# One pool of eight PSUM banks for a whole decoder layer, and a first pair of projections that steps through the contraction in lockstep

## The chip, the core and the metric

The kernel runs on one core of a Trainium2 chip. The metric is the device time of one execution in microseconds (us); lower is better. A core has TensorE (PE, with its weight loads shown apart as PEld), VectorE (DVE), ScalarE (ACT), GpSimd (POOL) and SyncE (SP, which issues most DMAs). Each engine runs its own list of instructions in order, and waits on semaphores for the others. PSUM, where PE writes its results, has eight banks; one bank holds 128 x 512 float32.

## The reference

One layer of a decoder with 512 tokens and 1024 model columns, in float32:

```python
x = x + 0.5 * swiglu(rms_norm(x, ffn1_norm_w), ffn1_w_gate, ffn1_w_up, ffn1_w_down)
h = rms_norm(x, mix_norm_w)
z, xbc, dt_raw, q, k, v = jnp.split(h @ w_in, split_idx, axis=-1)
xbc = jax.nn.silu(causal_dwconv(xbc, conv_w, conv_b))          # 1536 channels, 4 taps
xs, bm, cm = jnp.split(xbc, [1024, 1280], axis=-1)
y_ssd = ssd_chunked(xs, softplus(dt_raw + dt_bias), -exp(a_log), bm, cm, d_skip)
y_ssd = rms_norm(y_ssd * silu(z), ssd_norm_w)                  # per group of 512
q, k = rms_norm(q, q_norm_w), rms_norm(k, k_norm_w)            # 8 heads x 2 x 64
o = rms_norm(diff_attention(q, k, v, lam), attn_subln_w) * 0.8 # softmax(q1 k1) - lam softmax(q2 k2)
x = x + concat([y_ssd, o]) @ w_out
x = x + 0.5 * swiglu(rms_norm(x, ffn2_norm_w), ffn2_w_gate, ffn2_w_up, ffn2_w_down)
```

## The kernel before

Everything is held transposed, 128 channels on the partitions by 512 tokens. Every float32 product is made of three matmuls on operands split in a high and a low part (`mm3`: high x high, high x low, low x high). So a block of 128 weight rows by 512 tokens takes three matmuls, and a channel tile with its eight contraction blocks (k = 0 to 7) takes 24. Weights come in pieces (`piece`), in a fixed list: SP loads a piece into `raw` (three buffers), ACT or POOL makes `whi`, DVE makes `wlo` (four buffers each).

The stages follow each other in the program: feed-forward 1; the projections `xbc` (12 channel tiles, in six pairs, order 8 9, 10 11, 0 1, ... 6 7) with their convolution; the projections z and v mixed with the chunked state-space part (SSD); attention over eight heads mixed with the q and k projections; the output projection `wo`; feed-forward 2. The order on each engine is not that of the program alone: a list scheduler that simulates the engines picks among the instructions whose inputs and buffers are ready in its simulation, the earliest in the program first. So a buffer that is late in the simulation changes the order on the engines.

Steps that matter below:

- End of feed-forward 1. `down` makes the last sums `dn`; for each of eight blocks DVE adds them to x (L362), ACT and DVE make the split operands `xhm` and `xlm` (L236, L237) for the next projections, and POOL adds up squares in `accm` (L247). `finish` then turns `accm` into the norm's factors: PE sums (`psrm`), DVE computes a reciprocal root and a diagonal (L262), PE spreads it (`psbm`), ACT copies it to `rbcm`.
- PSUM. `psum_open` closes the pools in use and opens others on the same banks: eight single banks `P` in the feed-forwards; `A=2, M=2, J=2` in the mixer (an `A` tile is a pair of banks); `J=2, M=4, A=1` in attention.
- `xbc` (L170 to L172 with tile name xbc): the two channel tiles of a pair are written one after the other into one `A` tile. `conv_tile` on DVE (L473 `u`, L480, L482 `a`) empties it, ACT applies SiLU, PE transposes (`xt`, L494), ACT copies the result to `xs` (L496).
- SSD. Per chunk and group `ssd_a` makes the decay matrix `ab` (DMA, eight ReLU L648 and one Exp L649 on ACT, a multiply L653 on DVE), `ssd_o` makes the state's part, and `ssd_d` the diagonal part `pd` (L690), which reads `ab`.
- Attention. Per head `qk_tr` transposes q and k (six tiles qT, khT, klT), `att_s(h, i)` makes the scores `sc` of query block i and their softmax: DVE takes the maximum (L835), ACT exponentiates (L840), POOL and DVE combine the two maps into `pe` (L844, L845). `att_t(h, i)` transposes `pe` on PE (`at`, L853). `att_av` multiplies with v (`o`, 12 matmuls), `att_n` normalizes (`om`). Between these, `fill()` gives PE one part of the q and k projections of later heads (24 matmuls of 256 columns), or of `wo` at the end. In head 6 `y_split` reads the SSD result back and splits it: POOL makes `yh`, DVE makes `yl` (L903).

Of the kernel before, what the change touches and what calls it, by code (L numbers as in the profile page):

```python
# [8 lines left out]
F32 = mybir.dt.float32  # L9
# [29 lines left out]
def hymba_layer(ctx: ExitStack, tc: tile.TileContext, xT, gu1, dn1, wxbc, wdt, wz, wv, wqk,  # L39
                wo, gu2, dn2, cols, rows, out):  # L40
    nc = tc.nc
    V, S, G, PE = nc.vector, nc.scalar, nc.gpsimd, nc.tensor
# [1 line left out]
    const = ctx.enter_context(tc.tile_pool(name="const", bufs=1))  # L44
    wpool = ctx.enter_context(tc.tile_pool(name="wpool", bufs=4))
    dram = ctx.enter_context(tc.tile_pool(name="dram", bufs=1, space=DRAM))
    psum = {}

    def psum_open(**bufs):

        for cm, _ in reversed(list(psum.values())):
            cm.__exit__(None, None, None)
        psum.clear()
        for tag, n in bufs.items():
            cm = tc.tile_pool(name=f"ps{tag}", bufs=n, space=PSUM)
            psum[tag] = (cm, cm.__enter__())

    def pA(name):
        return psum["A"][1].tile([P, 2, T], F32, tag="A", name=name)

    def pM(name, dt=F32):
        return psum["M"][1].tile([P, T], dt, tag="M", name=name)

    def pJ(name):
        return psum["J"][1].tile([P, T], F32, tag="J", name=name)

    ctx.callback(psum_open)
    psum_open(P=8)
# [90 lines left out]
    def piece(ahead=2):  # L159
        i = taken[0]  # L160
        taken[0] += 1
        prep(i + 1 + ahead)
        return ready[i]

    def blk(w, k, width=P):
        return w[:, k * width:(k + 1) * width]

    def mm3(ps, w, k, xh, xl, start, stop):
        hi, lo = blk(w[0], k), blk(w[1], k)
        PE.matmul(ps, lhsT=hi, rhs=xh, start=start, stop=False)  # L170
        PE.matmul(ps, lhsT=hi, rhs=xl, start=False, stop=False)  # L171
        PE.matmul(ps, lhsT=lo, rhs=xh, start=False, stop=stop)  # L172
# [15 lines left out]
    identb = const.tile([P, P], BF16, name="identb")  # L188
# [30 lines left out]
    class Normed:  # L219
# [27 lines left out]
                (V if first else G).tensor_add(self.acc, sq, self.acc)  # L247

        def finish(self):
            pt = pP if "P" in psum else pM  # L250
            ps = pt(f"psr{self.name}")
            for j in range(NB):
                PE.matmul(ps[:, j:j + 1], lhsT=blk(self.acc, j), rhs=ones[:, 0:1], start=True, stop=True)
            self.v = tiny.tile([P, NB], F32, tag="nv", name=f"v{self.name}")
            V.tensor_scalar(self.v, ps[:, :NB], 1.0 / 1024, EPS, op0=ALU.mult, op1=ALU.add)
            self.r = tiny.tile([P, NB], F32, tag="nr", name=f"r{self.name}")
            rsqrt(self.r, self.v, [P, NB], "n")
            dg = self.acc.rearrange("p (a b) -> p a b", a=NB)
            pb = pt(f"psb{self.name}")
            sh = [P, NB, P]  # L260
            yield
            V.tensor_tensor(dg, ident.unsqueeze(1).to_broadcast(sh), self.r.unsqueeze(2).to_broadcast(sh),  # L262
                            op=ALU.mult)
            PE.matmul(pb, lhsT=ones, rhs=self.acc, start=True, stop=True)
            S.copy(self.rbc, pb)
            yield
# [146 lines left out]
    nm = [None]  # L413
# [7 lines left out]
    ffn(n1, x1, done1, "1", PARTS1, EARLY1)  # L421
    nm = nm[0]
    xpool_cm.__exit__(None, None, None)
    psum_open(A=2, M=2, J=2)


    mix_cm = tc.tile_pool(name="mix", bufs=1)
# [136 lines left out]
    for n, pair in enumerate(order):  # L564
        if n == 2:
            pt_dt = dt_proj()
            small_consts()
        ps = pA(f"xbc{n}")
        for i in range(2):
            w = piece()  # L570
            for k in range(KD):
                mm3(ps[:, i, :], w, k, nm.xh[:, k, :], nm.xl[:, k, :], k == 0, k == KD - 1)
            if n == 0 and i == 0:
                fin = nm.finish()
                next(fin)
            elif n == 0:
                next(fin)
        if n == 3:
            dt_finish(pt_dt)
        for t, dst in pend:  # L580
            conv_tr(t, dst)
        pend = [(t, conv_tile(t, ps[:, i, :])) for i, t in enumerate(pair)]
    last_conv = pend

    hr = const.tile([P, NB], F32, name="hr")
# [79 lines left out]
    def ssd_o(c, g, m, xdt, xdd, y):  # L665

        hs = slice(g * 8, g * 8 + 8)
        sh = [P, 8, 64]
        cs = slice(c * P, (c + 1) * P)
        pd = pds[c, g] = pA(f"pd{c}{g}")  # L670
        if c > 0:
            PE.matmul(pd[:, 1, :], lhsT=cT[:, g, cs], rhs=state[:, g, :], start=True, stop=True)
            yo = sb.tile(sh, F32, tag="yo", name="yo", bufs=1)
            V.tensor_tensor(yo, sview(pd[:, 1, :]), ea[:, c, hs].unsqueeze(2).to_broadcast(sh), op=ALU.mult)
            V.tensor_add(y, y, yo)
        if c < NB - 1:
            pst = pM(f"st{c}{g}")
            PE.matmul(pst, lhsT=btok[:, c, g, :], rhs=xdd.rearrange("p a b -> p (a b)"), start=True, stop=True)
            st = sview(state[:, g, :])
            if c == 0:  # L680
                S.copy(st, sview(pst))
            else:
                V.tensor_tensor(st, st, cdec[:, c, hs].unsqueeze(2).to_broadcast(sh), op=ALU.mult)
                V.tensor_add(st, sview(pst), st)

    def ssd_d(c, g, m, xdt, xdd, y):

        pd = pds.pop((c, g))
        for h in range(8):
            PE.matmul(pd[:, 0, h * 64:(h + 1) * 64], lhsT=m[:, h, :], rhs=xdt[:, h, :], start=True, stop=True)  # L690
        V.tensor_tensor(y, sview(pd[:, 0, :]), y, op=ALU.add)
        zt = sview(sz[:, c, g * 512:(g + 1) * 512])
        V.tensor_mul(zt, zt, y)
        S.activation(y, zt, AF.Square, accum_out=ssq[g][:, c:c + 1])
# [411 lines left out]
```

## Time and profile before

| | us |
|---|---|
| median of 3 runs (lowest, highest) | 1196.5 (1195.9, 1197.11) |
| the profiled execution | 1194.4 |
| its span, first to last instruction | 1192.3 |
| outside the span | 2.1 |
| PE busy | 1160.0 |
| DVE busy | 895.1 |
| ACT busy | 569.6 |

The profile shows one execution, 2.1 us below the median of the runs. Matmuls are pipelined: the duration of one overlaps the next, so a stretch of back-to-back matmuls is counted in matmuls per us, not in durations. Every row names the engine, the line of the kernel, the operation, what it writes and reads, and in brackets how long the engine was idle before it and what ended that.

### The profile page before, as it was taken

What the parts mean: (1) busy time and instruction counts of PE and PEld (TensorE: products, weight loads), DVE (VectorE), ACT (ScalarE), POOL (GpSimd) and SP (SyncE); (2) the same over time, 40 slices, a digit from 0 to 9 for tenths busy, and PEclk for the clock granted to TensorE, in tenths of its full rate; (3) what the DMA queues carried; (4) which work ended last, traced back from release to release, by engine and by line L of the source; (5) the groups of instructions that cost most, each with busy time, mean ns of one, the idle gap of its engine ahead of it and who ended that gap; (6) DMA issues with size and microseconds to landing.
All of it is one profiled execution on the core that took longest, in us unless ns stands there. A gap on an engine that the chain in (4) does not pass through costs nothing.

```text
span 1192.3 us, 18991 instructions
## 1 busy us (share of the span) xinstructions
PE 1160.0 (97%) x7483; PEld 1033.1 (87%) x7483; DVE 895.1 (75%) x1485; ACT 569.6 (48%) x991; POOL 155.2 (13%) x178
## 2 busy tenths in 40 slices
PE   8999999999998999999999998899999999999998
PEld 6889999999986788999988896688789999999997
DVE  6988787887675875976588988636599888787863
ACT  5433443343353448973366766735244444343331
POOL 1000000000022000000346656423000000000000
PEclk9999999999998999999999999999999999999999
DMA  6223333233253223423221103025213333333232
GB/s 231 89 76 98 100 108 99 92 111 106 89 186 127 77 90 107 142 89 110 88 70 48 60 19 124 27 63 211 80 62 105 108 111 98 110 107 102 96 108 84
DMA packets 42393, 119.56 MB, mean 100 GB/s; under 512 B 4608, under 2 KB 9920, under 8 KB 42304
## 3 DMA queue, kind: packets, MB, share of 16 engines
q1 hardware_dynamic: 41024, 114.15, 29.8%
q0 software_dynamic: 1280, 4.20, 1.0%
q8 instruction: 59, 0.97, 0.3%
q14 instruction: 30, 0.25, 0.1%
HBM read 112.00 MB, written 6.32 MB: 99 GB/s over the span
## 4 chain that ended last, share of the span: by engine, by line
PE 83%; DVE 8%; ACT 4%; issue 2%; POOL 1%; DMA 1%; SPq 0%; ACTq 0%; POOLq 0%; DVEq 0%
PE s L327 9%; PE s L326 9%; PE s L328 9%; PE dn L170 6%; PE dn L172 6%; PE dn L171 6%; PE gu L170 3%; PE gu L172 3%; PE gu L171 3%; PE wo L172 2%; PE wo L170 2%; PE wo L171 2%; PE xbc L170 2%; PE xbc L171 2%; PE xbc L172 2%
## 5 line engine op out<-in xcount | busy, mean ns | idle before, releaser
L128 ACT CAST whi<-raw 128x1024 fp32r<-128x1024 f32 (+2 forms) x204 | 176.6, 868 | 309.5 <-PE s L327 121.7
L129 DVE TENSOR_TENSOR wlo<-raw,whi 128x1024 fp32r<-128x1024 f32 (+3 forms) x225 | 226.5, 1010 | 113.4 <-ACT whi L128 102.0
L327 PE MATMUL s<-al,whi 128*128 128x256 f32 x952 | 265.0, 279 | 0.0
L326 PE MATMUL s<-ah,whi 128*128 128x256 f32 x952 | 263.4, 279 | 0.0
L328 PE MATMUL s<-ah,wlo 128*128 128x256 f32 x952 | 262.4, 279 | 0.0
L327 PEld LDWEIGHTS s<-al,whi 128*128 128x128 f32 x952 | 178.7, 188 | 2.1
L326 PEld LDWEIGHTS s<-ah,whi 128*128 128x128 f32 x952 | 178.3, 188 | 2.0
L328 PEld LDWEIGHTS s<-ah,wlo 128*128 128x128 f32 x952 | 177.1, 187 | 0.1
L128 ACT CAST whi<-tw 128x1024 fp32r<-128x1024 f32 x68 | 70.4, 1051 | 141.0 <-PE s L327 65.6
L170 PE MATMUL dn<-h,whi 128*128 128x512 f32 x352 | 137.5, 394 | 0.0
L172 PE MATMUL dn<-h,wlo 128*128 128x512 f32 x352 | 137.5, 392 | 0.0
L171 PE MATMUL dn<-h,whi 128*128 128x512 f32 x352 | 136.8, 389 | 0.0
L129 DVE TENSOR_TENSOR wlo<-tw,whi 128x1024 fp32r<-128x1024 f32 x68 | 82.0, 1220 | 2.9 <-ACT whi L128 2.8
L172 PEld LDWEIGHTS dn<-h,wlo 128*128 128x128 f32 x352 | 66.1, 188 | 14.6
L171 PEld LDWEIGHTS dn<-h,whi 128*128 128x128 f32 x352 | 66.1, 188 | 12.7
L170 PEld LDWEIGHTS dn<-h,whi 128*128 128x128 f32 x352 | 66.1, 188 | 12.2
L603 PE MATMUL qk<-whi,xhm 128*128 128x256 f32 x256 | 74.1, 289 | 0.3 <-DVE kf L781 0.3
L605 PE MATMUL qk<-whi,xlm 128*128 128x256 f32 x256 | 73.4, 287 | 0.0
L604 PE MATMUL qk<-wlo,xhm 128*128 128x256 f32 x256 | 73.1, 286 | 0.0
L362 DVE SCALAR_TENSOR_TENSOR x<-dn,x 128x512 f32<-128x512 f32 x64 | 44.1, 688 | 35.3 <-PE dn L172 34.8
L170 PE MATMUL gu<-xh,whi 128*128 128x512 f32 x160 | 65.0, 406 | 3.4 <-POOL whi L126 2.3
L172 PE MATMUL gu<-xh,wlo 128*128 128x512 f32 x160 | 63.7, 398 | 0.0
(293 smaller groups left out, 2529.1 us busy)
## 6 DMA issues: line engine op xcount, KB each, us to landing
raw<-in_gu SPq DMA_DIRECT2D x86, 512.0 KB, 3.5
raw<-in_dn SPq DMA_DIRECT2D x48, 384.0 KB, 3.1
raw<-in_wqk SPq DMA_DIRECT2D x16, 512.0 KB, 3.7
raw<-in_wxbc SPq DMA_DIRECT2D x12, 512.0 KB, 3.6
raw<-in_wo SPq DMA_DIRECT2D x10, 512.0 KB, 4.4
raw<-in_dn SPq DMA_DIRECT2D x16, 256.0 KB, 2.6
raw<-in_wz SPq DMA_DIRECT2D x8, 512.0 KB, 3.5
raw<-in_wv SPq DMA_DIRECT2D x8, 512.0 KB, 3.6
```

The lines of the kernel that those rows point to most:

```text
L128: S.copy(hi[:, a:b], raw[:, a:b])
L129: V.tensor_sub(lo[:, a:b], raw[:, a:b], hi[:, a:b].bitcast(F32))
L170: PE.matmul(ps, lhsT=hi, rhs=xh, start=start, stop=False)
L171: PE.matmul(ps, lhsT=hi, rhs=xl, start=False, stop=False)
L172: PE.matmul(ps, lhsT=lo, rhs=xh, start=False, stop=stop)
L326: PE.matmul(ps, lhsT=hi, rhs=ah[:, i, a], start=i == 0, stop=False)
L327: PE.matmul(ps, lhsT=hi, rhs=al[:, i, a], start=False, stop=False)
L328: PE.matmul(ps, lhsT=lo, rhs=ah[:, i, a], start=False, stop=i == 3)
L362: V.scalar_tensor_tensor(x[d], ps, 0.5, x[d], op0=ALU.mult, op1=ALU.add)
L603: PE.matmul(o, lhsT=xh, rhs=hi, start=k == 0, stop=False)
L604: PE.matmul(o, lhsT=xh, rhs=lo, start=False, stop=False)
L605: PE.matmul(o, lhsT=xl, rhs=hi, start=False, stop=k == KD - 1)
```

## The change

The pools `P`, `A`, `M`, `J` and their closing and opening are gone. One pool of eight single banks serves the whole program; `pM`, `pJ` and `pP` are now one function, and each pair of banks becomes two tiles. Three places follow from it: the scores of query blocks 2 and 3 are two tiles, so their maximum is taken by two reductions in place of one (16 more DVE instructions in all); the SSD tile `pd` becomes two tiles; `wo4` and `wo5` are two tiles. Apart from that, the first pair of `xbc` tiles steps through k in lockstep: for each k three matmuls of the one tile and three of the other. `finish` is split otherwise: `psrm` after the first pair, `psbm` after the first tile of the second pair, and the first pair's convolution comes after that.

```diff
-    psum = {}
-
-    def psum_open(**bufs):
...
-    def pA(name):
-        return psum["A"][1].tile([P, 2, T], F32, tag="A", name=name)
+    pspool = ctx.enter_context(tc.tile_pool(name="psum", bufs=8, space=PSUM))
 
     def pM(name, dt=F32):
-        return psum["M"][1].tile([P, T], dt, tag="M", name=name)
...
+        return pspool.tile([P, T], dt, tag="P", name=name)
+
+    pJ = pP = pM
...
-    psum_open(A=2, M=2, J=2)
...
-        ps = pA(f"xbc{n}")
+        ps = [pP(f"xbc{n}{i}") for i in range(2)]
+        if n == 0:
+            ws = [piece(), piece()]
+            for k in range(KD):
+                for p_, w in zip(ps, ws):
+                    mm3(p_, w, k, nm.xh[:, k, :], nm.xl[:, k, :], k == 0, k == KD - 1)
+            fin = nm.finish()
+            next(fin)
+            first_ps = ps
+            continue
         for i in range(2):
             w = piece()
             for k in range(KD):
-                mm3(ps[:, i, :], w, k, nm.xh[:, k, :], nm.xl[:, k, :], k == 0, k == KD - 1)
-            if n == 0 and i == 0:
-                fin = nm.finish()
+                mm3(ps[i], w, k, nm.xh[:, k, :], nm.xl[:, k, :], k == 0, k == KD - 1)
+            if n == 1 and i == 0:
                 next(fin)
-            elif n == 0:
-                next(fin)
+                pend0 = [(t, conv_tile(t, p_)) for t, p_ in zip(order[0], first_ps)]
...
-        pend = [(t, conv_tile(t, ps[:, i, :])) for i, t in enumerate(pair)]
+        pend = [(t, conv_tile(t, ps[i])) for i, t in enumerate(pair)]
+        if n == 1:
+            pend = pend0 + pend
...
-        pd = pds[c, g] = pA(f"pd{c}{g}")
+        pd = pds[c, g] = [pP(f"pd{c}{g}{i}") for i in range(2)[:2 if c else 1]]
...
         if i < 2:
-            ps = pM(f"sc{h}{i}").rearrange("p (a b) -> p a b", a=2)
+            ps2 = pM(f"sc{h}{i}").rearrange("p (a b) -> p a b", a=2)
+            ps = [ps2[:, t] for t in range(2)]
         else:
-            ps = pA(f"sc{h}{i}")
+            ps = [pM(f"sc{h}{i}{t}") for t in range(2)]
...
-        V.tensor_reduce(nmx, ps[:, :, :K], axis=AX, op=ALU.max, negate=True)
+        if i < 2:
+            V.tensor_reduce(nmx, ps2[:, :, :K], axis=AX, op=ALU.max, negate=True)
+        else:
+            for t in range(2):
+                V.tensor_reduce(nmx[:, t:t + 1], ps[t][:, :K], axis=AX, op=ALU.max, negate=True)
...
-    psum_open(J=2, M=4, A=1)
...
-    pa = pA("wo4")
-    wo_ps[4], wo_ps[5] = pa[:, 0, :], pa[:, 1, :]
+    wo_ps[4], wo_ps[5] = pJ("wo4"), pJ("wo5")
...
-    psum_open(P=8)
```

The scheduler, given other buffers, puts the mixer's instructions in another order on every engine. PE has the same matmuls in both. In its new order nearly every part stands as the program has it, where before parts were slipped between each other. Three places follow.

PE, start of the SSD part, from the last transpose of the convolution (`xt7`) to the first diagonal part (`pd00`, now `pd000`); z0_1 and z1_0 are halves of the projections z, `cb` and `st` small products of the SSD part. Before:

```order
L494 MATMUL xt7_4206<-ident_92,xst_4154 128x128 x4
L604 MATMUL z0_1_4277<-wlo_4067,xhm_3280 128x256
...
L644 MATMUL cb00_4250<-cT_3505,bT_3504 128x128
L678 MATMUL st00_4335<-xdd_4266,btok_3506 128x512
...
L644 MATMUL cb10_4377<-cT_3505,bT_3504 128x128
...
L678 MATMUL st10_4477<-xdd_4393,btok_3506 128x512
L603 MATMUL z1_1_4447<-whi_4165,xhm_3280 128x256
...
L644 MATMUL cb20_4515<-cT_3505,bT_3504 128x128
L690 MATMUL pd00_4334<-xdt_4263,ab_4248 128x64 x8
```

Now:

```order
L473 MATMUL xt7_4202<-ident_92,xst_4150 128x128 x4
L632 MATMUL cb00_4246<-cT_3495,bT_3494 128x128
L591 MATMUL z0_1_4273<-whi_4062,xhm_3280 128x256
...
L666 MATMUL st00_4331<-xdd_4262,btok_3496 128x512
...
L632 MATMUL cb10_4373<-cT_3495,bT_3494 128x128
L591 MATMUL z1_0_4346<-whi_4161,xhm_3280 128x256
...
L678 MATMUL pd000_4330<-xdt_4259,ab_4244 128x64 x8
L591 MATMUL z1_1_4443<-whi_4161,xhm_3280 128x256
```

Between `xt7` and the first `pd` stood 110 matmuls of z (14, 24, 24 and 48), two `st` and three `cb`; now 96 (48, 24 and 24), one `st` and two `cb`.

PE, first head, from its scores of query blocks 0 and 1 (sc00, sc01) to the transpose of its first softmax (`at00`); qk2_0 is a half of the projections of head 2. Before:

```order
L832 MATMUL sc01_5970<-cmask_106,identb_99 128x128
L830 MATMUL sc02_6046<-khT_5897,qT_5890 128x384
...
L832 MATMUL sc02_6046<-cmask_106,identb_99 128x128
...
L603 MATMUL qk2_0_6070<-whi_6066,xhm_3280 128x256
L604 MATMUL qk2_0_6070<-wlo_6067,xhm_3280 128x256
L605 MATMUL qk2_0_6070<-whi_6066,xlm_3281 128x256
L853 MATMUL at00_6042<-ident_92,pe_5962 128x128
```

Now:

```order
L821 MATMUL sc00_5942<-cmask_106,identb_99 128x128
L820 MATMUL sc01_5960<-klT_5915,qT_5901 128x256
L821 LDWEIGHTS identb_99
L821 MATMUL sc01_5960<-cmask_106,identb_99 128x128
L846 MATMUL at00_6032<-ident_92,pe_5952 128x128
L819 MATMUL sc020_6036<-khT_5887,qT_5880 128x384
```

The six matmuls of sc02 and 48 of qk2_0 that stood between the scores of block 0 and `at00` are now behind `at00`. In heads 1 to 5 the same stretch held 36, 43, 40, 36 and 47 matmuls of 256 columns, most of them of q and k projections, and the 12 of `o`; now 16, 9, 24, 11 and 24, and the 12.

DVE, head 6, from the maximum of its scores of block 0 (`nmx<-sc60`) to its first `pe`. Before:

```order
L835 TENSOR_REDUCE nmx_7870<-sc60_7863 128x2
L857 TENSOR_TENSOR atL_5676<-at53_7856,atH_5675 128x4x128
L836 TENSOR_TENSOR nmx_7870<-nmx_7870,qrs_7443 128x2
...
L842 RECIPROCAL l_7892<-l_7892 128x2
L836 TENSOR_TENSOR nmx_8004<-nmx_8004,qrs_7629 128x2
L845 SCALAR_TENSOR_TENSOR pe_7873<-pe_7873,l_7874 128x128
```

Now:

```order
L825 TENSOR_REDUCE nmx_7884<-sc60_7877 128x2
L850 TENSOR_TENSOR atL_5678<-at53_7870,atH_5677 128x4x128
...
L896 TENSOR_TENSOR yl_7988<-yt_7989,yh_7987 128x1024
...
L896 TENSOR_TENSOR yl_7988<-yt_7993,yh_7987 128x1024
L835 RECIPROCAL l_7906<-l_7906 128x2
L909 TENSOR_TENSOR ol2_7930<-oT_5676,oh2_7929 128x512
...
L896 TENSOR_TENSOR yl_7988<-yt_7997,yh_7987 128x1024
L838 SCALAR_TENSOR_TENSOR pe_7887<-pe_7887,l_7888 128x128
```

Three of the four `yl` now stand between the maximum and `pe`; before, all stood ahead of the maximum. On PE, 8 matmuls of 256 columns and the 12 of `o` stand between the scores of block 1 of head 6 and `at60`; before, 21 of `wo` (512 columns) and the 12. In head 7 PE now has 19 matmuls of `wo` and the 12 of `o` in this place, where before it had the 12 alone.

## Rows read from the trace of the kernel before

**Rows 1.** The page: busy time of each engine, share of the span, instructions.

```profile
PE 1160.0 (97%) x7483; PEld 1033.1 (87%) x7483; DVE 895.1 (75%) x1485; ACT 569.6 (48%) x991; POOL 155.2 (13%) x178
```

**Rows 2.** The waits of PE: who waited for whom, us in total, times, longest.

```profile
PE xbc L170 <- DVE x L362: 5.6, 1, 5.6
PE at L853 <- DVE pe L845: 3.5, 5, 1.1
PE wo L171 <- DVE yl L903: 2.7, 3, 1.4
PE at L853 <- DVE l L843: 2.6, 1, 2.6
...
PE qT L810 <- POOL qs L789: 2.2, 1, 2.2
PE sc L830 <- ACT pe L840: 1.5, 1, 1.5
...
PE at L853 <- ACT atH L856: 1.2, 1, 1.2
...
PE at L853 <- DVE klT L813: 0.8, 1, 0.8
PE pd L690 <- DVE ab L653: 0.8, 1, 0.8
```

**Rows 3.** The timeline from feed-forward 1 to xbc: start, us, instruction.

```profile
363.11 0.76 PE L170 MATMUL xbc<-xhm,whi 128*128 128x512 f32 x1 [5.57 <-DVE x L362]
364.02 1.76 DVE L237 SCALAR_TENSOR_TENSOR xlm<-x,col,xhm 128x512 fp32r<-128x512 f32 x1
374.40 0.95 PE L253 MATMUL psrm<-ones,accm 128*128 128x1 f32 x8
377.90 0.69 DVE L262 TENSOR_TENSOR accm<-ident,rm 128x512 f32<-128x512 f32 x1
```

**Rows 4.** Stretches: length, busy PE, PEld, DVE, ACT, POOL; clock; DMA, GB/s.

```profile
363.00:368.00 5.00, 4.89 (x12) 3.86 (x13) 2.78 (x2) 1.36 (x2) 3.71 (x6) 0.50 0.58 197
563.00:573.00 10.00, 10.00 (x88) 10.00 (x87) 2.15 (x4) 4.27 (x7) 0.00 (x0) 1.00 0.70 210
583.00:588.00 5.00, 4.95 (x32) 4.95 (x33) 2.38 (x9) 3.32 (x10) 1.93 (x2) 0.66 0.32 111
650.00:700.00 50.00, 47.28 (x370) 42.02 (x369) 45.71 (x95) 36.01 (x93) 32.33 (x31) 1.00 0.14 43
765.00:770.00 5.00, 5.00 (x18) 3.93 (x17) 1.99 (x5) 3.08 (x6) 2.28 (x3) 0.72 0.02 3
```

**Rows 5.** The timeline of PE from the last xt to the first pd.

```profile
452.02 0.60 PE L494 MATMUL xt<-ident,xst 128*128 128x128 f32 x4
470.05 2.00 PE L690 MATMUL pd<-xdt,ab 128*128 128x64 f32 x16 [0.77 <-DVE ab L653]
```

**Rows 6.** The timeline of DVE: block 0's maximum and pe, heads 0, 6, 7.

```profile
595.38 0.41 DVE L835 TENSOR_REDUCE nmx<-sc 128x2 f32<-128x256 f32 x1
...
600.90 0.35 DVE L845 SCALAR_TENSOR_TENSOR pe<-pe,l 128x128 f32<-128x128 f32 x1
...
741.40 0.42 DVE L835 TENSOR_REDUCE nmx<-sc 128x2 f32<-128x256 f32 x1
...
744.84 0.34 DVE L845 SCALAR_TENSOR_TENSOR pe<-pe,l 128x128 f32<-128x128 f32 x1
...
757.79 0.42 DVE L835 TENSOR_REDUCE nmx<-sc 128x2 f32<-128x256 f32 x1 [0.40 <-PE sc L832]
...
762.95 0.35 DVE L845 SCALAR_TENSOR_TENSOR pe<-pe,l 128x128 f32<-128x128 f32 x1
```

**Rows 7.** DVE's groups by shape: busy us, mean ns, idle before.

```profile
L129 DVE TENSOR_TENSOR wlo<-raw,whi 128x1024 fp32r<-128x1024 f32 x106 | 132.4, 1250 | 32.2 <-ACT whi L128 22.4 <-PE psb L264 4.8 <-POOL whi L126 3.3
...
L903 DVE TENSOR_TENSOR yl<-yt,yh 128x1024 fp32r<-128x1024 f32 x4 | 6.3, 1582 | 0.0
...
L835 DVE TENSOR_REDUCE nmx<-sc 128x2 f32<-128x512 f32 x8 | 5.4, 677 | 0.0
```

More of the change, by code (lines that the diff above doesn't have):

```diff
@@ L46, in hymba_layer @@
     dram = ctx.enter_context(tc.tile_pool(name="dram", bufs=1, space=DRAM))
-    psum = {}
-    def psum_open(**bufs):
[L51 to L56, printed above, removed]
-    def pA(name):
-        return psum["A"][1].tile([P, 2, T], F32, tag="A", name=name)
-    def pM(name, dt=F32):
-        return psum["M"][1].tile([P, T], dt, tag="M", name=name)
-    def pJ(name):
-        return psum["J"][1].tile([P, T], F32, tag="J", name=name)
-    ctx.callback(psum_open)
-    psum_open(P=8)
-    def pP(name):
-        return psum["P"][1].tile([P, T], F32, tag="P", name=name)
+    pspool = ctx.enter_context(tc.tile_pool(name="psum", bufs=8, space=PSUM))
+    def pM(name, dt=F32):
+        return pspool.tile([P, T], dt, tag="P", name=name)
+    pJ = pP = pM
     def ffn_plan(parts, early):
@@ L249, in finish @@
         def finish(self):
-            pt = pP if "P" in psum else pM
-            ps = pt(f"psr{self.name}")
+            ps = pP(f"psr{self.name}")
             for j in range(NB):
@@ L258, in finish @@
             dg = self.acc.rearrange("p (a b) -> p a b", a=NB)
-            pb = pt(f"psb{self.name}")
+            pb = pP(f"psb{self.name}")
             sh = [P, NB, P]
@@ L669, in ssd_o @@
         cs = slice(c * P, (c + 1) * P)
-        pd = pds[c, g] = pA(f"pd{c}{g}")
+        pd = pds[c, g] = [pP(f"pd{c}{g}{i}") for i in range(2)[:2 if c else 1]]
         if c > 0:
-            PE.matmul(pd[:, 1, :], lhsT=cT[:, g, cs], rhs=state[:, g, :], start=True, stop=True)
+            PE.matmul(pd[1], lhsT=cT[:, g, cs], rhs=state[:, g, :], start=True, stop=True)
             yo = sb.tile(sh, F32, tag="yo", name="yo", bufs=1)
-            V.tensor_tensor(yo, sview(pd[:, 1, :]), ea[:, c, hs].unsqueeze(2).to_broadcast(sh), op=ALU.mult)
+            V.tensor_tensor(yo, sview(pd[1]), ea[:, c, hs].unsqueeze(2).to_broadcast(sh), op=ALU.mult)
             V.tensor_add(y, y, yo)
@@ L689, in ssd_d @@
         for h in range(8):
-            PE.matmul(pd[:, 0, h * 64:(h + 1) * 64], lhsT=m[:, h, :], rhs=xdt[:, h, :], start=True, stop=True)
-        V.tensor_tensor(y, sview(pd[:, 0, :]), y, op=ALU.add)
+            PE.matmul(pd[0][:, h * 64:(h + 1) * 64], lhsT=m[:, h, :], rhs=xdt[:, h, :], start=True, stop=True)
+        V.tensor_tensor(y, sview(pd[0]), y, op=ALU.add)
         zt = sview(sz[:, c, g * 512:(g + 1) * 512])
@@ L824, in att_s @@
         if i < 2:
-            ps = pM(f"sc{h}{i}").rearrange("p (a b) -> p a b", a=2)
+            ps2 = pM(f"sc{h}{i}").rearrange("p (a b) -> p a b", a=2)
+            ps = [ps2[:, t] for t in range(2)]
         else:
-            ps = pA(f"sc{h}{i}")
+            ps = [pM(f"sc{h}{i}{t}") for t in range(2)]
         for t in range(2):
             qT, khT, klT = qkT[h][3 * t:3 * t + 3]
-            PE.matmul(ps[:, t, :kc], lhsT=blk(qT, i), rhs=khT[:, :kc], start=True, stop=False)
-            PE.matmul(ps[:, t, :kc], lhsT=blk(qT, i), rhs=klT[:, :kc], start=False, stop=False)
-            PE.matmul(ps[:, t, i * P:K], lhsT=identb, rhs=cmask, start=False, stop=True)
+            PE.matmul(ps[t][:, :kc], lhsT=blk(qT, i), rhs=khT[:, :kc], start=True, stop=False)
+            PE.matmul(ps[t][:, :kc], lhsT=blk(qT, i), rhs=klT[:, :kc], start=False, stop=False)
+            PE.matmul(ps[t][:, i * P:K], lhsT=identb, rhs=cmask, start=False, stop=True)
         rs = qk[h][i // 2][0][:, i % 2, :]
         nmx = tiny.tile([P, 2], F32, tag="nmx", name="nmx")
-        V.tensor_reduce(nmx, ps[:, :, :K], axis=AX, op=ALU.max, negate=True)
+        if i < 2:
[3 more added lines that the diff above has]
+                V.tensor_reduce(nmx[:, t:t + 1], ps[t][:, :K], axis=AX, op=ALU.max, negate=True)
         V.tensor_mul(nmx, nmx, rs[:, 0:2])
@@ L839, in att_s @@
         for t in range(2):
-            S.activation(pe[:, t, :K], ps[:, t, :K], AF.Exp, bias=nmx[:, t:t + 1], scale=rs[:, t:t + 1],
+            S.activation(pe[:, t, :K], ps[t][:, :K], AF.Exp, bias=nmx[:, t:t + 1], scale=rs[:, t:t + 1],
                          accum_out=l[:, t:t + 1])
@@ L1037, in hymba_layer @@
     xn_cm.__exit__(None, None, None)
-    psum_open(P=8)
     def done2(d):
```

## The prediction

> **What bounds the kernel now.** The page comes first: PE is busy for 1160.0 us of a span of 1192.3 [rows 1], DVE for 895.1. The matmuls are the same before and after, so the time can only change by three things: how long PE waits, at which clock it works, and whether another engine becomes the bound. The waits of PE come second [rows 2]. One stands out: 5.6 us of the first `xbc` matmul for DVE's last addition `x` (L362). The others that the change touches lie in attention (`at`, `sc`, `wo`) or at the seams ahead of it (`z`, `pd`, `qT`), each between 0.7 and 3.5 us. The stretches come third [rows 4]. In the 5 us from 363 the granted clock was 0.50, right behind the 5.57 us of idle PE; it was 0.66 behind the 2.20 us before `qT` and 0.72 behind the 2.60 us in the last head. So each long wait is paid twice: 5.0 x 0.50 = 2.5 us, 5.0 x 0.34 = 1.7 us and 5.0 x 0.28 = 1.4 us come on top. I price the clock behind a new long wait at 1.5 us, from the two shorter ones, with 0 and 2.5 as bounds. From 650 to 700, in the middle of attention, DVE is busy for 45.71 of 50 us: there it hardly has room.
>
> **The boundary: a gain of 8.1 us.** The first `xbc` tile is a pair of banks in a new pool, and gets them only when the last user of the old pool is done, DVE's `x` of block 7. Its operands for k = 0 were there long before. In one pool of single banks the two first tiles take the banks of the earliest `dn` sums, so PE goes on at 363.11 - 5.57 = 357.54 [rows 3]. There the lockstep matters: k = 7 is needed only after 42 matmuls of 512 columns. A matmul of 256 columns goes by in 10 / 88 = 0.114 us [rows 4], one of 512 in twice that, so k = 7 is reached at 357.54 + 42 x 0.228 = 367.1. Its `xlm` is ready at 364.02 + 1.76 = 365.8 [rows 3]. Nothing is left to wait for: -5.6 for the wait and -2.5 for the clock. If the clock fell all the same, the gain would be 5.6, which is the lower bound.
>
> **The norm's factors: a loss of 1.6 us.** From `psrm` to the end of DVE's diagonal there pass 377.90 + 0.69 - 374.40 = 4.2 us [rows 3]; in the new order of DVE two `wlo` of 128 x 1024 are slipped into that chain, 1.25 us each [rows 7]. PE has 24 matmuls of 512 columns in this time, 5.5 us; 4.2 + 2 x 1.25 - 5.5 gives +1.2, bounds 0 (the `wlo` find room in the chain's own pauses) and 2.6 (with the clock). The product of the time steps now stands directly behind its own result's copy on ACT; PE's waits for an operand made just before are 0.8 at `pd` and `klT` [rows 2], bounds 0 and 0.8, taken as +0.4.
>
> **The SSD's start: a loss of 4.4 us.** From the end of the last `xt` to the first `pd` there are 470.05 - 452.62 = 17.4 us [rows 5]. This is a chain through ACT and DVE (the decay matrix, its table and exponential, then `ab`), which the change leaves as it is. PE filled it with z, and waited 0.8 us at its end [rows 2]. Now 14 matmuls of z, one `st` and one `cb` fewer stand there: 14 x 0.114 = 1.6 us, and for the two others, by the 16 float32 matmuls of 64 columns that took 2.00 us [rows 5], 512 columns at 1.0 and 128 at 0.25. PE so waits 2.9 us more, 3.7 in all at `pd`, which is longer than the waits of 2.2 and 2.6 behind which the clock fell: +2.9 + 1.5 = +4.4. Bounds: 1.6 (only z counts, no clock) and 5.4 (2.9 + 2.5).
>
> **The first head: a loss of 5.0 us.** Block 0's softmax takes 600.90 + 0.35 - 595.38 = 5.9 us from its maximum to the end of `pe` [rows 6]. Before, 48 matmuls of projections and a third block's scores covered most of that, and PE waited 1.8 us (two of the five waits of `at` for `pe`, [rows 2]). Now `at00` stands directly behind `sc01`, whose six matmuls cover some 0.6 us. A wait of 5.9 - 0.6 = 5.3, less 1.8, with a clock of 1.5: +5.0. Bounds: 1.4 (the shortest chain of the eight heads, 3.8 us [rows 6], and no clock) and 6.0.
>
> **Heads 1 to 5: a loss of 0.6 us.** In head 7 before, the 12 matmuls of `o` alone stood in this place; its chain took 762.95 + 0.35 - 757.79 = 5.5 us [rows 6] and PE waited 2.6 [rows 2], so `o` and what goes with it cover 2.9. With 16, 9, 24, 11 and 24 more at 0.114 the covers are now 4.7, 3.9, 5.6, 4.2 and 5.6 us. The mean chain of the eight heads is 4.9; I take 5.2, between that and head 7's. Waits of 0.5, 1.3, 0, 1.0 and 0 give 2.8 against 1.0 before (3.5 less 1.8 in head 0 and 0.7 in head 6, [rows 2]). I count the 1.2 us for `atH` as absorbed, since PE now stands still a little earlier and the late engines catch up: +1.8 - 1.2 = +0.6. Bounds: -2.2 (no such wait left) and +1.8.
>
> **Head 6: a loss of 2.4 us.** Three `yl` of 1.58 us [rows 7] now stand on DVE between the maximum and `pe`: a chain of 4.9 + 4.7 = 9.6 against a cover of 2.9 + 8 x 0.114 = 3.8, a wait of 5.8 and a clock of 1.5. The waits that it replaces are 2.7 for `yl`, 1.5 for `pe` at `sc` [rows 2] and 0.7 for `pe` at `at`: 7.3 - 4.9 = +2.4. Bounds: -0.2 (a chain of 3.8, as this head had [rows 6], and no clock) and +3.4.
>
> **The tail: a gain of 4.8 us.** In head 7 the 19 matmuls of `wo` now lie between scores and transposes: 19 x 0.228 = 4.3 and 2.9 cover 7.2 us against a chain of 5.5. The 2.6 and 0.8 us [rows 2] and the clock's 1.4 [rows 4] go.
>
> **Taken as nothing.** The 16 split maxima: one of 512 takes 0.68 [rows 7], two of 256 take 0.41 to 0.42 each [rows 6], so a split costs 0.15 and all of them 2.3 us of DVE, hidden behind PE as long as PE waits for block 0 and not for blocks 2 and 3; on the path it would be +2.3. The Trainium skill (Perfetto Trace Analysis, Optimizing Scalar/DVE Operations) has some 125 ns of overhead for a DVE instruction on PSUM and advises larger operations where the engine is saturated: by an estimate from it 16 x 0.125 = 2.0 us, a loss if DVE is the bound. `qT` keeps its 2.2 us, bounds -2.2 and +1.7. Feed-forward 2 and the projections v and q, k run as before.
>
> **The sum.** -8.1 + 1.2 + 0.4 + 4.4 + 5.0 + 0.6 + 2.4 - 4.8 = +1.1. The profiled execution took 1194.4 us, so 1195.5; the median of the runs shown, 1196.5, lies 2.1 above that execution. The forecast is 1197.6 us: what is gained at the seams is given back where the transposes now stand close behind the softmax.
>
> **The rivals.** *B, faster: the chains get shorter.* With eight banks free in any stage, scores and projections need not wait for a pair or for a pool, DVE and ACT get their input sooner, and the softmax takes its shortest time of 3.8 us in every head. No new wait then lasts long enough for the clock. The terms become -8.1, 0, +0.4, +2.9, +1.4 (head 0), -2.2 (heads 1 to 5), -0.2 and -4.8: -10.6, or 1185.9 us. For it: one head of the eight did have 3.8 [rows 6], and the largest wait of all was one for banks. Against it: the other waits of [rows 2] are all for an operand that DVE, ACT or POOL makes, not for a bank. The Trainium skill (Perfetto Trace Analysis, Optimization Strategy) says that a repeated gap on the engine that should be busy "can mean there isn't enough SBUF/PSUM for the next tile to be allocated"; by that rule B would be the case. The trace agrees at one place, the 5.57 us of the boundary, which do not repeat.
>
> *C, slower: DVE becomes the bound in attention.* It is busy for 91% of the time from 650 to 700 [rows 4], and in the new order each chain starts closer to the work it must share DVE with. With chains 1.5 us longer than taken the waits of heads 1 to 5 are 2.0, 2.8, 1.1, 2.5 and 1.1, or 6.7 more; heads 0 and 6 get 1.5 each, and two of the waits reach the clock, 3.0. That is +12.7 on the forecast, 1210.3 us. It decides from a chain of some 5.5 us on, where 0.3 us in each of seven heads already makes the kernel slower by 0.2%. Against it: while PE waits, DVE works off what is late.
>
> *D, no change at the boundary.* If another operand of the first pair is late (DVE is working without a pause there), the 8.1 us stay: 1205.7 us. Against it: the weights' `wlo` are made two pieces ahead.
>
> **How the numbers follow.** A measurement of this kernel can tell about 0.2%, 2.4 us, from no change. The forecast has a chance of 0.52, B 0.27, C 0.13, D 0.08. The forecast's own range is 1192 to 1203, from its bounds at half their width; about 0.11 of its 0.52 lie below 1194.1, 0.25 within 2.4 us of 1196.5, and 0.16 above 1198.9. B is faster, C and D are slower: 0.38 faster, 0.25 the same, 0.37 slower. The range reaches from B's time to two thirds of the way to C's, 1185 to 1206; it leaves out C's upper half, a part of D and what lies below B, together some 2 in 10.
>
> **What would show it.** The wait of `xbc` for `x` is gone from the list of PE's waits, and the clock at 358 to 368 is 1.0 (otherwise D). New waits stand at `psbm` (about 1.2 us), `pd` (3.7), the first `at` (5.3) and the `at` of head 6 (5.8), the latter three with a clock of 0.5 to 0.7 behind them. The last head shows no wait over 1 us. If the waits of `at` sum to under 7 us and no clock falls in attention, B holds; if heads 1 to 5 wait over 6 us, C. The prediction is wrong above all if PE waits for a bank at a place that the order does not show, since tiles now come free in one ring, or if the chain ahead of `pd` follows PE instead of ACT.

## The result, and the profile after

The changed kernel takes 1209.7 us (median of 4 runs, 1209.4 to 1210.8) against 1196.2 us before in the same rounds: a ratio of 1.012, 95% interval 1.0107 to 1.0132. The forecast was 1197.6, the range ended at 1206. The span grew from 1192.3 to 1207.7 us.

The page of the changed kernel, busy times:

```profile
PE 1165.2 (96%) x7483; PEld 1040.2 (86%) x7483; DVE 890.7 (74%) x1501; ACT 571.8 (47%) x993; POOL 155.0 (13%) x178
```

Against [rows 1] DVE is busy for 4 us less although it has 16 instructions more. PE has as many matmuls as before. So the loss is in waits and in the clock. PE's waits after (who waited for whom, us in total, times, longest):

```profile
PE at L846 <- DVE pe L838: 17.9, 6, 5.5
PE at L846 <- DVE l L836: 6.2, 1, 6.2
PE pd L678 <- DVE ab L641: 4.7, 1, 4.7
...
PE o L861 <- DVE atL L850: 1.9, 2, 0.9
PE qT L798 <- POOL qs L777: 1.4, 1, 1.4
...
PE klT L798 <- POOL kl L780: 0.9, 1, 0.9
PE klT L798 <- ACT pe L833: 0.7, 1, 0.7
PE psdtT L494 <- ACT dtr L491: 0.7, 1, 0.7
PE khT L798 <- ACT kh L779: 0.6, 1, 0.6
PE qk L591 <- ACT pe L833: 0.2, 1, 0.2
```

The reader sees three things beside [rows 2]. The wait of `xbc` for `x` is gone, and so are the 2.6 us of the last head and the 2.7 us of `wo` for `yl`. The wait at `pd` is 4.7 us where it was 0.8. And the transposes `at` wait 24.1 us for the softmax, in seven of eight heads, where these waits summed to 6.1.

The stretch behind the boundary, where the wait is gone, and those behind the new waits (length, busy PE, PEld, DVE, ACT, POOL, then the granted clock, DMA share, GB/s):

```profile
363.00:368.00 5.00, 5.00 (x26) 4.13 (x25) 2.45 (x3) 1.69 (x5) 3.37 (x6) 1.00 0.53 165
...
455.00:460.00 5.00, 2.40 (x11) 2.40 (x12) 1.65 (x2) 4.99 (x15) 0.00 (x0) 0.61 0.34 105
460.00:465.00 5.00, 5.00 (x24) 5.00 (x25) 3.45 (x5) 2.78 (x6) 0.00 (x0) 0.50 0.29 105
465.00:470.00 5.00, 5.00 (x30) 4.04 (x29) 2.61 (x5) 4.93 (x16) 0.00 (x0) 0.87 0.02 5
...
583.00:588.00 5.00, 4.17 (x23) 4.18 (x24) 3.39 (x8) 2.25 (x6) 2.74 (x3) 0.50 0.12 48
...
598.00:603.00 5.00, 2.53 (x10) 1.92 (x11) 3.48 (x17) 3.20 (x12) 0.85 (x2) 0.65 0.36 105
603.00:608.00 5.00, 5.00 (x29) 4.73 (x29) 2.41 (x6) 1.79 (x5) 1.86 (x2) 0.67 0.01 3
650.00:655.00 5.00, 4.19 (x15) 2.77 (x16) 3.80 (x12) 1.89 (x6) 0.62 (x2) 0.66 0.28 104
675.00:680.00 5.00, 2.79 (x10) 1.61 (x10) 4.83 (x15) 1.62 (x6) 2.31 (x2) 0.80 0.63 210
680.00:685.00 5.00, 5.00 (x34) 4.14 (x33) 1.59 (x6) 3.65 (x10) 3.36 (x3) 0.86 0.01 3
700.00:705.00 5.00, 2.33 (x16) 1.77 (x15) 4.40 (x13) 4.16 (x15) 2.09 (x3) 1.00 0.53 171
750.00:755.00 5.00, 1.97 (x8) 1.38 (x8) 3.97 (x9) 0.52 (x3) 4.24 (x4) 0.50 0.77 226
755.00:760.00 5.00, 5.00 (x19) 3.49 (x18) 4.92 (x12) 3.54 (x7) 0.00 (x0) 0.85 0.48 133
```

At the boundary the clock is 1.00, where it was 0.50. Elsewhere busy PE times what the clock lacks of 1 is, as an estimate, what the clock took. Behind `pd` that is 2.40 x 0.39 + 5.00 x 0.50 + 5.00 x 0.13 = 4.1 us, in head 0 it is 2.5, in heads 2 and 3 it is 1.4 and 1.3, and in head 6 it is 1.7. Head 4's wait of 2.67 us is not followed by a lower clock (1.00 from 700).

### The profile page after: what moved, and what is told of

Its sections match the earlier page's. It is cut to its first block, busy times and chain, and to the rows that moved or that the text cites. A ratio compares the mean times of both kernels' runs of the same rounds, so it can differ in the third digit from the quotient of the medians.

```text
span 1207.7 us, 18994 instructions
## 1 busy us (share of the span) xinstructions
PE 1165.2 (96%) x7483; PEld 1040.2 (86%) x7483; DVE 890.7 (74%) x1501; ACT 571.8 (47%) x993; POOL 155.0 (13%) x178
## 4 chain that ended last, share of the span: by engine, by line
PE 87%; DVE 6%; ACT 3%; issue 2%; POOL 1%; DMA 1%; SPq 0%; ACTq 0%; POOLq 0%; DVEq 0%
PE s L307 9%; PE s L306 9%; PE s L308 9%; PE dn L151 7%; PE dn L153 7%; PE dn L152 7%; PE gu L151 3%; PE gu L153 3%; PE gu L152 3%; PE wo L151 2%; PE wo L153 2%; PE wo L152 2%; PE xbc L151 2%; PE xbc L153 2%; PE xbc L152 2%
## 5 line engine op out<-in xcount | busy, mean ns | idle before, releaser
L153 PEld LDWEIGHTS dn<-h,wlo 128*128 128x128 f32 x352 | 66.1, 188 | 14.6
L591 PE MATMUL qk<-whi,xhm 128*128 128x256 f32 x256 | 77.9, 304 | 0.2 <-ACT pe L833 0.2
```

What stands on the lines that cost most here:

```text
L591: PE.matmul(o, lhsT=xh, rhs=hi, start=k == 0, stop=False)
```

## The experiments

**Which stage.** Two theories stood at the start. The order theory: PE's `at` and `pd` now stand too close behind the chains that feed them, so the loss is in the SSD part and in attention. The ring theory: a pool of single banks itself costs. In the first run the boundary and the `xbc` stage are the changed ones, and the SSD part and attention have the pools and maxima of before.

```diff
     last_conv = pend
+    psum_open(A=2, M=2, J=2)
...
+    psum_open(J=2, M=4, A=1)
     fillers += [qk_proj(h) for h in range(1, 8)]
```

> The changed boundary and xbc stage alone; the SSD part and attention run with the pools of before, and their maxima are not split. Order theory (the loss of the changed kernel is that PE's transposes and diagonal products now stand too close behind their softmax and decay chains, in the SSD part and in attention): PE's order in attention is that of before, so only the gain at the boundary is left, about 7.8 us, and some 2 to 4 us of waits at pd, for more z stands ahead of it: 1185 to 1190 us. Ring theory (a pool of single banks is itself what costs, by waits for banks or by the clock): the xbc stage has such a pool too, so the gain at the boundary is given back within the stage, 1194 to 1198 us.

Measured: 1187.9 us, ratio to before 0.9944 (0.9926 to 0.9961). PE's waits in it:

```profile
PE at L867 <- DVE pe L859: 6.8, 6, 3.0
...
PE wo L173 <- DVE yl L917: 2.5, 3, 1.4
...
PE z L614 <- ACT xs L497: 1.5, 1, 1.5
```

The wait at the boundary is not among them, `at` waits 6.8 us, where it was 6.1 before, and `pd` not at all. The ring theory falls for the `xbc` stage. The boundary is a real gain of some 7 us (0.56%), which the rest of the change loses again with 13.5 more.

The second run puts the pool of eight single banks into attention alone:

```diff
-    psum_open(J=2, M=4, A=1)
+    psum_open(P=8)
```

> Before, with the one pool of eight single banks (and the split maxima) from the attention on and nothing else changed. Order theory: the loss that the trace of the changed kernel shows in attention, 17 us more of waits and low clock than before, comes with it: 1208 to 1215 us. If the loss in attention is only a consequence of what happens earlier (other stages shift the weights and the DMAs): 1195 to 1200 us.

Measured: 1213.5 us, 1.0144 (1.0121 to 1.0166), as the order theory said, but in part for a reason that it did not name:

```profile
PE at L860 <- DVE pe L852: 10.8, 4, 3.9
PE qk L605 <- DVE kf L783: 9.9, 1, 9.9
PE at L860 <- DVE l L850: 6.2, 1, 6.2
```

The 9.9 us are the price of the switch between the two pools at this place, where the new pool's first tile waits for the last reader of the old ones; the changed kernel has no switch there. (That `kf` is such a reader is concluded: `qk` does not read `kf`. The kernel before opens other pools at this place too, and PE waits only 2.2 us there, for an operand; why its banks were free in time was not followed up.) What speaks for the order theory is the 10.8 and 6.2 us (and 2.4 more in one row that is left out) of `at`, 19.4 in all. The time of this run alone shows nothing.

**More work in front of the waits.** The changed kernel, with its one pool and its split maxima, gets another program order in attention: the scores of block 2 and one part of the projections ahead of the first transpose.

```diff
-        att_t(h, 0)
         att_s(h, 2)
...
         fill()
-        att_t(h, 1)
+        att_t(h, 0)
         att_s(h, 3)
+        att_t(h, 1)
```

> The changed kernel with its one pool and its split maxima, but in the program of attention the scores of query block 2 and one part of the next projections stand ahead of the first transpose, so PE has 6 to 9.7 us of work between the scores of block 0 and their transpose, where the changed kernel has 0.2 to 5.1 (7.1 in the last head). Order theory: the waits of at for pe (24 us in the changed kernel) fall to under 5 us and the low clock behind them goes: 1189 to 1195 us. Split theory (16 more maxima on an engine without room make the softmax late, wherever the transposes stand): DVE's work is the same, the waits move to another place, and the time stays at 1204 to 1210 us.

Measured: 1194.5 us, 0.9995 (0.9982 to 1.0008), 15 us less than the changed kernel. `at` waits for no softmax in it any more; another wait has come up (the row of `pd` is left from the changed kernel):

```profile
PE om L872 <- ACT osq L865: 9.9, 7, 2.3
PE pd L678 <- DVE ab L641: 4.7, 1, 4.7
```

The split theory falls. The same for the SSD part, two more parts of z ahead of `pd`:

```diff
     ops = ssd_a(*steps[0])
-    unit(2)
+    unit(4)
```

> The changed kernel with two more parts of z (48 matmuls, 5.5 us) in the program ahead of the first diagonal product pd; attention as in the changed kernel, but for small shifts. Order theory: the wait of 4.7 us at pd and the low clock behind it (5 us by the stretches) go: 1199 to 1203 us. Rival (the chain of ACT ahead of pd grows with the two parts, whose tanh and copies stand in ACT's list too, or a later pd waits instead): 1207 to 1211 us.

Measured: 1203.8 us, 1.0074 (1.0053 to 1.0095), 6 us less than the changed kernel and just above the order theory's range. The wait at `pd` is gone, and no later `pd` waits. Attention keeps its waits (22.9 us of `at` for `pe`). Both together:

> The changed kernel with both orders: scores of block 2 and one part of the projections ahead of the first transpose of a head, and two more parts of z ahead of the first pd. Order theory: the two gains, 15 us of the one and 6 us of the other, lie in different stages and add up: 1186 to 1191 us. Rival (what is removed in the SSD part turns up again in attention, whose DVE work then starts earlier against the same end): 1192 to 1196 us.

Measured: 1181.3 us, 0.9891 (0.9878 to 0.9905), 28 us less than the changed kernel. The rival is out, but the order theory's range ended at 1186 too: the two gains of 15 and 6 us are worth 7 us more together than their sum, and why is not shown. Then `om` one part later:

```diff
         att_s(h, 2)
-        if h > 0:
-            att_n(h - 1)
...
         fill()
         att_t(h, 0)
+        if h > 0:
+            att_n(h - 1)
```

> As the kernel with both orders, but the sum over squares om of the head before stands behind one more part of the projections and the first transpose, where PE in the run with the attention's order alone waited 9.9 us for ACT's squares. Order theory: most of these waits go: 1180 to 1186 us. Rival (PE then waits for the same late ACT and DVE at the next place): 1186 to 1191 us, as with both orders alone.

Measured: 1179.9 us, 0.9867 (0.9846 to 0.9889), just below what the order theory said. Of `om`'s waits 0.6 us are left of 10.6, but the gain is 1.4 us, less than the two intervals can tell apart. PE's waits together fall only from 21.2 to 15.1 us: part of them turned up at other places, as the rival said.

**Why the order was better with fewer banks.** The changed program, unchanged, but in attention the eight single banks are in three pools:

```diff
+    psum_open(J=2, M=4, S=2)
     fillers += [qk_proj(h) for h in range(1, 8)]
...
-            ps = [pM(f"sc{h}{i}{t}") for t in range(2)]
+            ps = [pS(f"sc{h}{i}{t}") for t in range(2)]
```

> The changed kernel, program and split maxima unchanged, but attention gets its eight single banks in three pools of 2, 4 and 2 (projections; transposes and small scores; scores of blocks 2 and 3). By the order the scarcer banks let later work slip ahead of the transposes as before: 6.7 to 11.3 us of PE work between scores and transpose of block 0 in heads 0 to 6, 3.1 in head 7. Order theory: the loss in attention goes, the loss of the SSD part stays: 1192 to 1199 us. Theory that single banks or split maxima are what costs in attention: 1204 to 1210 us.

Measured: 1195.1 us, 0.9994 (0.9979 to 1.0009). PE's longest waits:

```profile
PE qk L612 <- DVE kf L790: 10.1, 1, 10.1
PE pd L699 <- DVE ab L662: 4.7, 1, 4.7
PE at L867 <- DVE pe L859: 2.4, 1, 2.4
```

It pays 10.1 us for the switch and keeps the 4.7 us at `pd`, and is yet 14.6 us faster than the changed kernel, since the waits of `at` fall from 24.1 to 4.2 us. Nothing in the program was written in another order: with a bank short, the scheduler let the parts of the projections pass the transposes. Nor is it the pause at the switch that did it: the run with one pool in attention has such a pause (9.9 us) and keeps 19.4 us of `at`. So it was the scarcity that gave the kernel before its work in front of the transposes.

**The split maxima alone**, in the kernel before:

```diff
-        V.tensor_reduce(nmx, ps[:, :, :K], axis=AX, op=ALU.max, negate=True)
+            for t in range(2):
+                V.tensor_reduce(nmx[:, t:t + 1], ps[:, t, :K], axis=AX, op=ALU.max, negate=True)
```

> The kernel before with only the maxima of query blocks 2 and 3 taken by two reductions; pools as before, and PE's work between the scores of block 0 and their transpose stays at 6.6 to 8.5 us in heads 0 to 6, by the order. Split theory (16 more reductions on a DVE without room are a good part of the loss): 1199 to 1204 us. Order theory (they cost 2.3 us of DVE that PE's work hides): within 2 us of before, 1193 to 1198 us.

Measured: 1192.4 us, 0.9978 (0.9966 to 0.9989). They cost nothing; the small gain can't be put down to them, since the order moved with them too.

**The lockstep alone** taken back:

```diff
-            for k in range(KD):
-                for p_, w in zip(ps, ws):
+            for p_, w in zip(ps, ws):
+                for k in range(KD):
```

> The changed kernel with its first two xbc tiles one after the other, each with all its k, in place of the lockstep; all else, the order too, is the same. Lockstep theory: the first tile needs k = 6 and 7 after 18 and 21 matmuls, 1 and 3 us ahead of their low parts; PE waits 3 to 4 us and loses some 2 us of clock: 1213 to 1217 us. Rival (the gain at the boundary came from the pool alone, and the first tiles' banks are all that PE waited for): 1208 to 1211 us.

Measured: 1209.4 us, 1.0113 (1.0098 to 1.0128), the same as the changed kernel. The order was not quite taken back: the scheduler puts 19 matmuls of the first tile, then 3 of the second, 2 of the first, and so on by itself. PE waits once, for 0.39 us:

```profile
363.66 0.50 PE L152 MATMUL xbc<-xlm,whi 128*128 128x512 f32 x1 [0.39 <-DVE xlm L218]
```

The lockstep theory falls: the free banks were enough.

**The longer softmax.** The chains from maximum to `pe` had grown in heads 1 to 5, from 4.8 us in the mean to 6.0. One of them, head 1 of the changed kernel, in the timeline:

```profile
618.66 0.42 DVE L825 TENSOR_REDUCE nmx<-sc 128x2 f32<-128x256 f32 x1 [0.66 <-PE sc L821]
...
621.94 1.41 POOL L837 TENSOR_SCALAR pe<-pe,l 128x128 f32<-128x128 f32 x1 [0.40 <-DVE l L835]
621.96 1.23 DVE L110 TENSOR_TENSOR wlo<-raw,whi 128x1024 fp32r<-128x1024 f32 x1
...
623.32 1.04 POOL L107 TENSOR_SCALAR whi<-raw 128x1024 fp32r<-128x1024 f32 x1
623.38 1.12 DVE L838 SCALAR_TENSOR_TENSOR pe<-pe,l 128x128 f32<-128x128 f32 x1
```

POOL's step lies beside DVE's `wlo` and takes 1.41 us, and DVE's `pe` lies beside POOL's `whi` and takes 1.12. The groups of POOL's step in the kernel before, and in the changed one:

```profile
L844 POOL TENSOR_SCALAR pe<-pe,l 128x128 f32<-128x128 f32 x7 | 2.6, 371 | 15.8 <-DVE l L842 15.8
```

```profile
L837 POOL TENSOR_SCALAR pe<-pe,l 128x128 f32<-128x128 f32 x7 | 7.3, 1047 | 3.8 <-DVE l L835 3.8
```

So ACT was given the high parts of the weights in attention:

```diff
-    pool_hi[0] = True
+    pool_hi[0] = False
     for h in range(8):
```

> The changed kernel, but in attention ACT and not POOL makes the high parts whi of the weights; POOL's list then holds no conversion of 1 to 2 us ahead of its step of the softmax. PE's order between scores and transposes is nearly the same (3.6 to 5.1 us of work in heads 1 to 6). Conversion theory (the softmax of heads 1 to 6 became longer, 5.3 to 9.6 us against 3.8 to 5.5 before, since POOL's and DVE's conversions of weights stand within it): the waits of at for pe fall by 4 us or more, 1201 to 1206 us. Rival (ACT, with 15 more conversions of 1 us, makes the exponentials late by as much): 1208 to 1213 us.

Measured: 1195.6 us, 1.0000 (0.9984 to 1.0015): 14 us less than the changed kernel, with nearly its order on PE, far more than the 4 us expected. The chains of heads 1 to 5 are 4.9 us again; one of them, and below it the waits of `at`:

```profile
611.56 0.42 DVE L825 TENSOR_REDUCE nmx<-sc 128x2 f32<-128x256 f32 x1 [0.63 <-PE sc L821]
...
615.64 0.38 POOL L837 TENSOR_SCALAR pe<-pe,l 128x128 f32<-128x128 f32 x1 [2.21 <-DVE l L835]
616.05 0.35 DVE L838 SCALAR_TENSOR_TENSOR pe<-pe,l 128x128 f32<-128x128 f32 x1 [0.39 <-POOL pe L837]
```

```profile
PE at L846 <- DVE l L836: 11.1, 3, 6.2
PE at L846 <- DVE pe L838: 6.3, 2, 5.5
```

Heads 0 and 6 wait as before the edit (5.5 and 6.2 us), heads 1 to 5 for 6.2 us together where it was 12.4. The rest of the 14 us was not placed. That seemed to make the conversions the cause and not the order. A control decides: the same edit in the kernel before.

> Control: the kernel before with ACT in place of POOL for the high parts of the weights in attention, as in the run that did this to the changed kernel and took 14 us from it. Cover theory (a longer softmax costs only where PE's work behind the scores does not cover it; the kernel before has 7 to 8 us of such work in heads 0 to 5): there is nothing to win, 1193 to 1199 us. Rival (POOL's conversions cost in any order, and the changed kernel's loss has nothing to do with its order): 1187 us or less.

Measured: 1186.3 us, 0.9920 (0.9900 to 0.9939). The cover theory, by which nothing was to be won there, was wrong. POOL's conversions cost the kernel before 9.8 us as well. There they stood in the softmax of later query blocks: DVE's step `pe` on 384 columns (575 to 800), in the kernel before and with the edit:

```profile
L845 DVE SCALAR_TENSOR_TENSOR pe<-pe,l 128x384 f32<-128x384 f32 x8 | 8.9, 1107 | 2.1 <-POOL pe L844 2.1
```

```profile
L845 DVE SCALAR_TENSOR_TENSOR pe<-pe,l 128x384 f32<-128x384 f32 x8 | 5.9, 741 | 2.9 <-POOL pe L844 2.9
```

With them on ACT in both, the changed kernel is 1195.6 - 1186.3 = 9.3 us slower than before, with them on POOL 13.5. So about 4 of the 13.5 us, give or take 3 by the intervals, belong to the conversions' falling into the softmax of block 0, and 9 do not. And last, the edit on top of both new orders:

> The one pool with both new orders and the later om, and with ACT making the high parts in attention. Cover theory: with 8 to 9 us of work behind the scores of heads 1 to 6 the shorter softmax is worth little, 1177 to 1182 us. Rival (the conversions cost in any order): 1172 us or less.

Measured: 1171.7 us, 0.9802 (0.9779 to 0.9824), the rival's time. It is the fastest kernel here, and PE's longest wait is that for the first weights; the others are at most about half as long:

```profile
PE gu L151 <- POOL whi L107: 2.5, 1, 2.5
...
PE khT L798 <- ACT kh L779: 1.2, 1, 1.2
```

## Why the prediction was wrong

The mechanism was right: the boundary's wait and its low clock went, the tail's waits went, and new waits stand where transposes and diagonal products follow their chains closely. The waits themselves were right within 1 us at `pd` (3.7 forecast, 4.7 measured), in head 0 (5.3 and 5.5) and in head 6 (5.8 and 6.2); at `psbm` none came. Two things were mis-sized, heads 1 to 5 above all and the clock behind the waits. Term by term, with the clock by busy PE as above:

| term | forecast | measured |
|---|---|---|
| boundary | -8.1 | -8.0: wait 5.6, clock 4.89 x 0.50 = 2.4 of [rows 4] |
| norm's factors | +1.6 | +0.7: only `psdtT` waits, `psbm` does not |
| SSD's start | +4.4 | +6.9: waits 4.7 less 1.9 before, clock 4.1 |
| qT, khT, klT | 0 | +1.9: waits 2.9 less 2.2, clock 2.9 (578 to 593, of which one stretch is shown) less 1.7 |
| head 0 | +5.0 | +6.2: wait 5.5 less 1.8, clock 2.5 |
| heads 1 to 5 | +0.6 | +14.4: `at` 12.4 less 1.0, other waits 0.3, clock 2.7 |
| head 6 | +2.4 | +3.0: wait 6.2 less 4.9, clock 1.7 |
| tail | -4.8 | -4.8: head 7 has no wait |

They sum to +20.3, where the span grew by 15.4. The pages place most of the 5 us between: PE's idle time, span less busy, grew by 10.2 us, where the table has 11.9 of waits (the waits for the first weights, which it leaves out, fell by 1.1), and its busy time grew by 5.2, where the table has 8.4 for the clock. So some 3 us are in the estimate of the clock.

**Heads 1 to 5** is the step that failed: +0.6 us in the sum, +14.4 measured. The forecast set a chain of 5.2 us against covers of 3.9 to 5.6 and found 2.8 us of waits. The chains were 5.8, 5.6, 7.8, 5.6 and 5.3 us, 4.1 more in all, for the weights' conversions fell into them. And the covers, chain less wait, were 4.4, 3.0, 3.6, 2.9 and 3.7, 6.4 less in all. The covers were the larger part: with the conversions on ACT and chains of 4.9 us, shorter than forecast, these heads still waited 6.2 us. What was wrong in them: the 2.9 us of `o`, taken from head 7 of [rows 6], were too much, since PE does part of that work before the maximum begins. In head 2 the scores of block 0 are done by 643.3; the timeline of POOL and DVE there:

```profile
642.91 1.29 POOL L780 TENSOR_TENSOR kl<-kf,kh 128x512 fp32r<-128x512 f32 x1
642.97 2.30 DVE L110 TENSOR_TENSOR wlo<-raw,whi 128x1024 fp32r<-128x1024 f32 x1 [1.49 <-POOL whi L107]
645.20 0.41 DVE L825 TENSOR_REDUCE nmx<-sc 128x2 f32<-128x256 f32 x1
```

The maximum stands behind a `wlo` and starts 2 us late; in heads 3 to 5 it starts 1.8, 2.2 and 1.7 us late, behind a `wlo` in head 4 and behind DVE's other work in heads 3 and 5. In heads 2 and 4 the stretch also holds a wait of its own (`o` for `atL`, 0.95 us). A wait that is the small difference of two numbers of 5 us was given as if each were exact. With covers within 1.3 us of the chains in five heads, 1 us more of the one and 1 us less of the other are 10 us.

**The clock's price** was mis-sized: 1.5 us behind each new wait, where `pd` paid 4.1, head 0 paid 2.5, and heads 2 and 3, for which none was counted, 1.4 and 1.3. Over the span the mean granted clock fell from 0.992 to 0.983.

**The absorbed wait.** 1.2 us for `atH` were counted as won back, since the late engines catch up while PE stands still. This wait is gone, but others came in its place: the waits of heads 1 to 5 that are not of `at` for `pe` summed to 2.9 us after, 2.6 before.

Rival C had the right sign and the right stage, longer chains in attention, and at 1210.3 us nearly the time. But its reason, DVE as the bound, is not shown: from 650 to 700 DVE was busy for 45.71 of 50 us [rows 4] and is now for 36.0, and the 16 maxima cost nothing in a run of their own; what was right in it is that single conversions on DVE and POOL stand in front of the softmax and in it. That its number came so close is in part luck. Rival D is out.

Rival B saw something true, and the ground given against it, that all other waits of [rows 2] are for an operand, was misread. Besides `sc` for `pe` and `at` for `klT`, 1.5 and 0.8 us in [rows 2], the kernel before has:

```profile
PE z L603 <- ACT sz L620: 0.7, 1, 0.7
PE khT L810 <- DVE atL L857: 0.7, 1, 0.7
...
PE qk L603 <- DVE kf L781: 0.3, 1, 0.3
```

In all five the waiting matmul reads nothing that the named instruction makes, while that instruction reads a PSUM tile: they are, by this argument, waits for banks, 4.0 us beside the boundary's 5.6. In the changed kernel two such are left (`klT` and `qk` for `pe`), 0.9 us. So the one pool did what B expected of it; what B missed is that the waits for operands then doubled, from some 19 to 38 us. With the banks free and the order mended, the same pool is faster than before by 1.3%. The rule of the Trainium skill named beside it (Perfetto Trace Analysis, Optimization Strategy), that a repeated gap can mean too little PSUM for the next tile, fits these 9.6 us in what they wait for, though they are no one gap that repeats. In attention fewer banks gave the better order (`at` 4.2 against 24.1 us).

## What to carry to other kernels

A pool that is short of buffers also sets the order in which a list scheduler lets work pass; who frees the buffers must put into the program the order that the shortage gave, here more projections between softmax and transpose. Where PE's work behind a chain is within 1 us of the chain's length, price the stage with the chain 1 us longer, in every repeat, and the new waits with the low clock that can follow them, here up to 4.1 us. And a control of the kernel before belongs to every edit that seems to explain a loss: here it took 9.8 of 14 us from the explanation.

## What the runs showed of the hardware

POOL's step of the softmax takes 0.37 us by itself and 1.41 us beside DVE's subtraction `wlo`; it ends at 623.35, 0.16 us after `wlo` does. DVE's `pe` beside POOL's `whi`, which starts 0.06 us earlier, ends 0.14 us after it, and the `wlo` of head 2, 0.06 us behind POOL's `kl`, takes 2.30 us and ends 1.07 us after `kl` does. The Trainium skill (SBUF — State Buffer, SBUF: two separate sides) says that GpSimd and VectorE share a port pair as an exclusive lock: of a VectorE operation with two inputs in SBUF and a GpSimd operation that reads SBUF, the one that starts first has it for its whole length. The trace agrees that one is done behind the other; in the first of these pairs the one that waits, POOL, starts 0.02 us ahead by the record, so who came first can't be read so finely. Moving 13 conversions of 1.2 us from POOL to ACT was worth 9.8, 14.1 and 8.2 us in three orders of the same kernel. Where in the kernel before the 9.8 us came from is shown in part: its waits fell from 28.3 to 23.4 us and DVE's steps on 384 columns became shorter; the rest is open.

Behind idle times of PE of 2.6 to 6.2 us, and behind three of 1.4, 0.6 and 0.9 us close together (`qT`, `khT`, `klT`), the granted clock went down to between 0.50 and 0.87 in the stretches shown and took 1.3 to 4.1 us. The longest wait (6.2, head 6) did not pay the most, and of two of nearly one length, 2.57 us in head 2 and 2.67 in head 4, only the first was followed by a lower clock (0.66 against 1.00).
